# Encoder layer on one core: the down projection's quadrant sums by accumulating DMA, the residual on VectorE, four rows of the final norm in another place

## The chip, the cores and the metric

One core of a Trainium2 chip runs the whole program in one launch. The metric is device time in microseconds (us): the median of several executions. A profile is one such execution, taken by the hardware profiler. Its engines are PE (TensorE, the matmuls), DVE (VectorE), ACT (ScalarE), POOL (GpSimd) and SP (SyncE, which here only issues transfers). Transfers (DMA) run on 16 DMA engines that all queues share; the queue names SPq, ACTq and POOLq say who issued a transfer.

## The reference

One encoder layer on a sequence of 1024 positions and 1024 channels, in float32: a layer norm, a Fourier mixer, a residual with layer norm, a gated MLP with a convolution of three taps over positions, and again a residual with layer norm. The part that the change touches is the end:

```python
def conv_ffn(x, w_up, conv_w, conv_b, w_down):
    h = depthwise_conv(x @ w_up, conv_w, conv_b)
    g, v = jnp.split(h, 2, axis=-1)
    return (jax.nn.silu(g) * v) @ w_down

h = layer_norm(DEEPNORM_ALPHA * h + mix, ln_tok_g, ln_tok_b)
ffn = conv_ffn(h, ff_w_up, ff_conv_w, ff_conv_b, ff_w_down)
h = layer_norm(DEEPNORM_ALPHA * h + ffn, ln_ffn_g, ln_ffn_b)
```

The gated product has 1024 positions and 2816 features; `w_down` is 2816 x 1024. The kernel's outputs are these 1024 x 1024 numbers.

## The kernel before, in words

The up projection makes the gated features in 22 blocks of 128 (index `j`). Each block is convolved by VectorE (`tap`, L1042), passed through SiLU on ScalarE, multiplied with its value half by GpSimd (`conv_done`, L1074) and stored to DRAM in the tensor `gd` by a transfer from ScalarE's queue (`store`).

The down projection multiplies the gated features (A: 1024 positions x 2816 features) by the weight (B: 2816 x 1024). A and B are cut into quadrants, two halves of the features by two halves of positions or of output channels, and the four quadrant products are made with seven multiplications in place of eight, of sums and differences of quadrants. These are the seven stages `s` = 0 to 6. A stage runs over `NK` = 11 feature blocks of 128, taken in pairs: `NB` = 6 steps `b`, the last with one block only (`span(b)`). `order` lists the 42 pairs (s, b).

For each pair there are four steps:

- `down_load` fetches the quadrant pieces that the stage needs, a tile of 128 partitions x 2 x 512 each (512 KB), by transfers on SP's queue (L1089): from `gd` into tiles `qa`, from the weight into tiles `qw`. The running sums of A and of B live in the tiles `sst[b]` and `tst[b]`.
- `down_sums` forms the stage's sums by elementwise instructions (L1129): the weight's on VectorE, the activation's on GpSimd for even `b` and on VectorE for odd `b`.
- `down_prep` splits each sum into a high and a low part for three reduced-precision matmul passes: a cast on ScalarE (L175, tiles `ga` and `wb`), then a subtraction on VectorE (L172).
- `down_mm` runs the matmuls: 4 position blocks x 2 feature blocks x 3 passes (L181, L183, L185), 24 for a full pair, into four PSUM banks `dn`. Stages 0 to 5 add up in two sets of four banks. After a stage, `down_out` adds the set's present content into or out of the residual tiles `acc` on VectorE (L1303), so that each product reaches all the outputs it belongs to.

The steps run ahead of each other by hand: at the turn `n` the loop loads pair n + 3, prepares pair n + 2 and multiplies pair n. Instructions of PE, VectorE, ScalarE and GpSimd run on each engine in the order in which the program writes them; a transfer on SP's queue waits until its tile is free. Nearly all large tiles are taken from one pool of `N4` = 46 buffers.

In `extra` other work is laid between the stages: the convolution of the last feature block, the load of the eight residual tiles `acc` (`load_acc`, 128 rows each), and `residual2`, which scales and shifts each of them, 384 columns on VectorE and 640 on GpSimd (L1171, L1172).

Stage 6 is the last product. It runs row block by row block (banks `dl`), so that rows 0 to 3 can be finished one at a time. Rows 4 to 7 are complete after stage 5. `last_row` makes a row's mean and variance (`bn_aggr`), its reciprocal root on GpSimd (L214, a power) and calls `finish`, which normalizes one part of the columns on VectorE and another on ScalarE and GpSimd (L1265, L1272, L1273) and stores the row. Before, `last_row(4 + rb)` stands after the matmuls of row `rb`, ahead of `last_row(rb)`.

Of the kernel before, what the change touches and what calls it, by code (L numbers as in the profile page):

```python
# [10 lines left out]
F32 = mybir.dt.float32  # L11
# [10 lines left out]
DFF = 2816  # L22
NF = DFF // P
HALF = 512
NFREQ = 514
EPS = 1e-5
ALPHA = 2.0 ** 0.25
# [73 lines left out]
def layout(inp):  # L101
    a = {}
    x = inp["x"][0]
    a["x"] = np.concatenate([x[fold_order()].reshape(8, P, D), x[row_order()].reshape(8, P, D)[1::2]])
    a["winT"] = inp["fn_w_in"][0].T.reshape(G, GD, D)
    wo = inp["fn_w_out"][0].reshape(G, GD, D)
    a["w1"] = wo[:, 1:64].reshape(4, 126, D)
    a["w2"] = wo[:, :64:-1].reshape(4, 126, D)
    e = wo[:, 0:65:64].reshape(16, D)
    we = np.zeros((80, D), e.dtype)  # L110
    for r in (0, 32, 64):
        we[r : r + 16] = e
    a["we"] = we
    up = inp["ff_w_up"][0].reshape(2, KT // 2, P, 2, NF, P)
    a["wup"] = up.transpose(4, 3, 2, 0, 1, 5).reshape(NF, 2, P, D)
    a["wd"] = inp["ff_w_down"][0].reshape(NF, P, D)
    cw = np.concatenate([inp["ff_conv_w"][0], inp["ff_conv_b"][0][None]], axis=0).reshape(4, 2, NF, P)
    a["cols"] = np.concatenate(
        [
            inp["emb_ln_g"].reshape(KT, P).T,  # L120
            inp["fn_b_in"][0].reshape(G, P).T,
            inp["ln_tok_g"][0].reshape(KT, P).T,
            inp["ln_tok_b"][0].reshape(KT, P).T,
            cw.transpose(3, 2, 1, 0).reshape(P, NF * 8),
        ],
        axis=1,
    )
    a["rows"] = np.stack(
        [
            inp["emb_ln_g"],  # L130
            inp["emb_ln_b"],
            inp["fn_b_out"][0],
            inp["ln_tok_g"][0],
            inp["ln_tok_b"][0],
            inp["ln_ffn_g"][0],
            inp["ln_ffn_b"][0],
        ]
    ).reshape(7, 1, D)
    a.update(constants())
    return {k: np.ascontiguousarray(v) for k, v in a.items()}  # L140
# [3 lines left out]
def encoder_layer(ctx: ExitStack, tc: tile.TileContext, a, out: bass.AP):  # L144
# [20 lines left out]
    def raw(ap):  # L165
        return ap.bitcast(F32)
# [7 lines left out]
    def split(hi, lo, src, eng=nc.vector):  # L174
        nc.scalar.copy(out=hi, in_=src)  # L175
        lows(lo, src, hi, eng)
# [860 lines left out]
    prep(0, (4, 3))  # L1037
    prep_b(3, full, ks=(0,))

    gd = dram.tile([NF, P, SEQ], F32, name="gd")  # L1040
    def tap(t, c, w, lo, hi, sh, wi):
        nc.vector.scalar_tensor_tensor(  # L1042
            out=t[:, lo:hi],
# [7 lines left out]
    spill, ct = {}, {}  # L1051

    def store(j):
        nc.scalar.dma_start(out=gd[j], in_=spill.pop(j))

    def conv_taps(j, v, part=range(4)):
        c = cc[j][v]
# [16 lines left out]
        nc.gpsimd.tensor_tensor(out=tg, in0=tg, in1=tv, op=ALU.mult)  # L1074
        spill[j] = tg

    NK = NF // 2
    NB = (NK + 1) // 2
    lo_c, hi_c = hs
    quads, sst, tst, dops = {}, {}, {}, {}  # L1080

    def span(b):
        return min(2, NK - 2 * b)

    def quad(name, src, half, b, c):
        n = span(b)
        t = t4([P, 2, 512], F32, name)
        f0 = half * NK + 2 * b
        nc.sync.dma_start(out=t[:, 0:n], in_=src[f0 : f0 + n, :, c].rearrange("k p c -> p k c"))  # L1089
        return t  # L1090

    def act_quad(i, k, b, s):
        return quad(f"qa{s}{b}", gd, k, b, hs[i])

    def wgt_quad(k, j, b, s):
        return quad(f"qw{s}{b}", a["wd"], k, b, hs[j])

    def down_load(s, b):
        q = quads[s, b] = {}
        if s == 0:  # L1100
            q["a"] = act_quad(0, 0, b, s)
            tst[b] = wgt_quad(0, 0, b, s)
        elif s == 1:
            sst[b] = act_quad(1, 0, b, s)
            q["a"] = act_quad(1, 1, b, s)
            q["b"] = wgt_quad(0, 1, b, s)
        elif s == 2:
            q["a"] = act_quad(0, 0, b, s)
            q["b"] = wgt_quad(1, 1, b, s)
        elif s == 3:  # L1110
            q["a"] = act_quad(1, 1, b, s)
            q["b"] = wgt_quad(0, 0, b, s)
        elif s == 4:
            q["a"] = act_quad(0, 1, b, s)
            q["b"] = wgt_quad(1, 1, b, s)
        elif s == 5:
            q["a"] = act_quad(1, 1, b, s)
            q["b"] = wgt_quad(1, 0, b, s)
        else:
            q["a"] = act_quad(0, 1, b, s)  # L1120
            q["b"] = wgt_quad(1, 0, b, s)

    def down_sums(s, b):
        n = span(b)
        q = quads[s, b]
        ea = nc.gpsimd if b % 2 == 0 else nc.vector

        def tt(eng, o, x, y, op):
            eng.tensor_tensor(out=o[:, 0:n], in0=x[:, 0:n], in1=y[:, 0:n], op=op)  # L1129

        if s == 0:
            return q["a"], tst[b]
        if s == 1:
            tt(ea, sst[b], sst[b], q["a"], ALU.add)
            tt(nc.vector, tst[b], q["b"], tst[b], ALU.subtract)
            return sst[b], tst[b]
        if s == 2:
            tt(ea, sst[b], sst[b], q["a"], ALU.subtract)
            tt(nc.vector, tst[b], q["b"], tst[b], ALU.subtract)
            return sst[b], tst[b]  # L1140
        if s == 3:
            tt(ea, q["a"], q["a"], sst[b], ALU.subtract)
            tt(nc.vector, q["b"], tst[b], q["b"], ALU.subtract)
            return q["a"], q["b"]
        if s == 4:
            tt(ea, q["a"], q["a"], sst[b], ALU.subtract)
            return q["a"], q["b"]
        if s == 5:
            tt(nc.vector, q["b"], q["b"], tst[b], ALU.subtract)
            return q["a"], q["b"]  # L1150
        return q["a"], q["b"]

    def down_prep(s, b):
        n = span(b)
        xa, xb = down_sums(s, b)
        g = [t4([P, 2, 2, 256], F32R, f"ga{s}{b}{l}") for l in range(2)]
        w = [t4([P, 2, 512], F32R, f"wb{s}{b}{l}") for l in range(2)]
        split(g[0][:, 0:n], g[1][:, 0:n], xa[:, 0:n].rearrange("p k (j u) -> p k u j", u=2))
        split(w[0][:, 0:n], w[1][:, 0:n], xb[:, 0:n])
        dops[s, b] = g, w  # L1160

    acc = []
# [3 lines left out]
        nc.sync.dma_start(out=z, in_=h1d[i])  # L1166
        acc.append(z)

    def residual2(i):
        for eng, c in ((nc.vector, slice(0, 384)), (nc.gpsimd, slice(384, 1024))):  # L1170
            eng.tensor_tensor(out=acc[i][:, c], in0=acc[i][:, c], in1=tokg[:, c], op=ALU.mult)  # L1171
            eng.tensor_tensor(out=acc[i][:, c], in0=acc[i][:, c], in1=tokb[:, c], op=ALU.add)  # L1172

    held = {1: 3, 2: 1}
    for j in range(NF):
# [155 lines left out]
    def extra(s, b):  # L1331
        if s == 0:
            if b == 0:
                store(NF - 2)
                conv_taps(NF - 1, 1)
            elif b == 1:
                conv_done(NF - 1)
                for i in range(4):
                    load_acc(i)
                residual2(0)  # L1340
            elif b == 2:
                store(NF - 1)
                for i in range(4, 8):
                    load_acc(i)
                residual2(1)
            else:
                residual2(b - 1)
        elif s == 1:
            if b == 0:
                residual2(5)  # L1350
                down_out(0)
            elif b == 1:
                residual2(6)
            elif b == 2:
                residual2(7)
        elif b == 0 and s < 6:
            down_out(s - 1)
        if s == 5 and b == 1:
            for i in range(4):
                half_stats(i, 1)  # L1360
            for i in range(4, 8):
                half_stats(i, 1)

    for n, (s, b) in enumerate(order[: 6 * NB]):
        if s < 2 and b == 0:
            banks[s] = [bank(f"dn{s}{rb}") for rb in range(4)]
        if n + 3 < len(order):
            down_load(*order[n + 3])
        if n + 2 < len(order):
            down_prep(*order[n + 2])  # L1370
        down_mm(s, b, range(4), banks[s % 2], slice(0, 512), s < 2 and b == 0, b == NB - 1)
        extra(s, b)
        if (s, b) == (4, 0):
            ffg, ffb = row(5, "ffg"), row(6, "ffb")
    for n in range(6 * NB + 2, len(order)):
        if n + 1 < len(order):
            down_load(*order[n + 1])
        down_prep(*order[n])
    for rb in range(4):
        z = acc[4 + rb][:, hs[0]]  # L1380
        nc.vector.tensor_tensor(out=z, in0=z, in1=banks[1][rb], op=ALU.add)
        half_stats(4 + rb, 0)
    for rb in range(4):
        pieces = (slice(0, 512),) if rb < 3 else (slice(0, 256), slice(256, 512))
        for pi, c in enumerate(pieces):
            bk = bank(f"dl{rb}{pi}")
            for b in range(NB):
                down_mm(6, b, (rb,), {rb: bk[:, 0 : c.stop - c.start]}, c, b == 0, b == NB - 1)
            if pi == 0:
                last_row(4 + rb)  # L1390
            z = acc[rb][:, c]
            nc.vector.tensor_tensor(out=z, in0=z, in1=bk[:, 0 : c.stop - c.start], op=ALU.add)
            nc.vector.bn_stats(out=s6[rb][:, 0 if pi == 0 else 2], in_=z)
# [21 lines left out]
```

## Time and profile before

| | us |
|---|---|
| median of three runs | 902.02 (901.75 to 903.17) |
| profiled execution, its own time | 900.76 |
| span in the profile, first to last instruction | 899.0 |
| PE busy | 819.8 |
| VectorE busy | 784.1 |
| GpSimd busy | 450.2 |
| ScalarE busy | 374.1 |
| first weight load and last matmul start of stages 0 to 5 | 635.7 and 854.0 |

Busy time is a sum over the span. Matmuls are pipelined and their ends are modelled, so a busy PE may still run below its peak; the number of matmuls in a stretch, and the clock that it was granted, say more. In the page's slices each digit is the busy share of a fortieth of the span in tenths. A group's row gives the line, engine, operation, output and inputs, count, busy time and mean duration, and behind the second bar the idle time of the engine ahead of these instructions and who ended it.

### The profile page before, as it was taken

How to read it: one execution, taken by the hardware profiler on the slowest of the kernel's cores; microseconds unless marked ns; L12 is line 12 of the kernel's file. 1: busy time of each engine (PE TensorE's matmuls, PEld its weight loads, DVE VectorE, ACT ScalarE, POOL GpSimd, SP SyncE). 2: the span in 40 equal slices, each digit the busy share in tenths (PEclk: the TensorE clock that was granted, in tenths of full speed). 3: DMA queues.
4: the chain of work that ended last, by engine and by line, in shares of the span. 5: the costliest groups of instructions: out<-in, count | busy, mean ns of one | idle time of the engine just before them, and what ended most of it. 6: DMA issues, size and time to landing. Idle time of an engine off the chain costs nothing.

```text
span 899.0 us, 10396 instructions
## 1 busy us (share of the span) xinstructions
PE 819.8 (91%) x3803; PEld 671.4 (75%) x3803; DVE 784.1 (87%) x1000; ACT 374.1 (42%) x572; POOL 450.2 (50%) x254
## 2 busy tenths in 40 slices
PE   8985989967899999999999999999974899999993
PEld 7874968866688788888888888888752677788883
DVE  5998798999897998887888888787999999989975
ACT  4524563564354444444444343444511234244511
POOL 4579597977814633455433455431199222210056
PEclk9997989988999999999999999999997899999998
DMA  9206531221122322222322222336793355477412
GB/s 360 102 1 147 153 140 48 94 94 48 47 71 94 94 94 71 71 70 80 118 84 70 71 71 71 105 103 195 269 331 124 125 175 195 146 259 270 150 71 117
DMA packets 42196, 112.35 MB, mean 125 GB/s; under 512 B 3673, under 2 KB 4569, under 8 KB 42145
## 3 DMA queue, kind: packets, MB, share of 16 engines
q1 hardware_dynamic: 38192, 97.92, 31.8%
q10 hardware_dynamic: 3168, 11.54, 3.2%
q0 software_dynamic: 784, 2.23, 1.0%
q8 instruction: 30, 0.49, 0.2%
q14 instruction: 22, 0.17, 0.1%
HBM read 91.75 MB, written 19.92 MB: 124 GB/s over the span
## 4 chain that ended last, share of the span: by engine, by line
PE 51%; DVE 16%; issue 3%; POOL 3%; ACT 2%; DMA 0%; POOLq 0%; ACTq 0%; DVEq 0%
PE by L181 6%; PE by L185 6%; PE by L183 6%; PE bz L181 4%; PE bz L183 4%; PE bz L185 4%; PE bx L181 4%; PE bx L183 4%; PE bx L185 4%; DVE wb L172 4%; PE dn L183 3%; PE dn L185 3%; PE dn L181 3%; DVE ga L172 2%; DVE t L1042 2%
## 5 line engine op out<-in xcount | busy, mean ns | idle before, releaser
L1074 POOL TENSOR_TENSOR t<-t,t 128x1024 f32<-128x1024 f32 x22 | 54.6, 2483 | 241.1 <-DVE t L1042 198.3
L1042 DVE SCALAR_TENSOR_TENSOR t<-c,cols,t 128x1 f32<-128x1 f32 (+2 forms) x264 | 141.8, 585 | 3.5 <-ACT t L1064 0.5
L181 PE MATMUL dn<-wb,ga 128*128 128x512 f32 x264 | 107.2, 406 | 13.6 <-DVE ga L172 13.6
L183 PE MATMUL dn<-wb,ga 128*128 128x512 f32 x264 | 107.5, 407 | 10.6 <-DVE wb L172 10.5
L181 PE MATMUL by<-b,a 128*128 128x512 f32 (+1 forms) x268 | 106.3, 397 | 3.6 <-DVE c L918 3.6
L185 PE MATMUL dn<-wb,ga 128*128 128x512 f32 x264 | 106.0, 402 | 0.0
L185 PE MATMUL by<-b,a 128*128 128x512 f32 (+1 forms) x268 | 105.6, 394 | 0.0
L183 PE MATMUL by<-b,a 128*128 128x512 f32 (+1 forms) x268 | 105.5, 393 | 0.0
L172 DVE TENSOR_TENSOR a<-s,a 128x512 fp32r<-128x512 f32 x85 | 87.5, 1030 | 18.4 <-ACT a L869 18.4
L175 ACT CAST ga<-qa 128x1024 fp32r<-128x1024 f32 (+1 forms) x42 | 44.1, 1050 | 84.0 <-DVE qa L1129 58.9
L181 PE MATMUL bz<-b,a 128*128 128x512 f32 (+1 forms) x180 | 71.4, 397 | 3.5 <-DVE a L172 3.5
L1129 POOL TENSOR_TENSOR qa<-qa,qa 128x1024 f32<-128x1024 f32 x12 | 35.0, 2912 | 78.1 <-DMA qa<-gd 66.2
L183 PE MATMUL bz<-b,a 128*128 128x512 f32 (+1 forms) x180 | 71.1, 395 | 2.9 <-DVE b L172 2.9
L181 PE MATMUL bx<-b,a 128*128 128x512 f32 (+1 forms) x192 | 72.2, 376 | 1.3 <-ACT c L985 1.3
L183 PE MATMUL bx<-b,a 128*128 128x512 f32 (+1 forms) x192 | 71.9, 374 | 0.0
L185 PE MATMUL bx<-b,a 128*128 128x512 f32 (+1 forms) x192 | 71.9, 374 | 0.0
L181 PEld LDWEIGHTS dn<-wb,ga 128*128 128x128 f32 x264 | 51.1, 193 | 27.7 <-issue 8.3
L183 PEld LDWEIGHTS dn<-wb,ga 128*128 128x128 f32 x264 | 51.1, 193 | 27.0 <-DVE wb L172 15.6
L185 PE MATMUL bz<-b,a 128*128 128x512 f32 (+1 forms) x180 | 71.1, 395 | 0.0
L172 DVE TENSOR_TENSOR a<-wr,a 128x512 fp32r<-128x512 f32 x64 | 70.4, 1102 | 0.4 <-ACT a L869 0.4
L172 DVE TENSOR_TENSOR wb<-qw,wb 128x1024 fp32r<-128x1024 f32 (+1 forms) x42 | 65.9, 1569 | 0.5
L918 DVE TENSOR_TENSOR c<-bz,c 128x512 f32<-128x512 f32 x44 | 30.4, 691 | 39.0 <-PE bz L185 38.3
(332 smaller groups left out, 2036.6 us busy)
## 6 DMA issues: line engine op xcount, KB each, us to landing
wr<-wup SPq DMA_DIRECT2D x44, 512.0 KB, 4.1
qa<-gd SPq DMA_DIRECT2D x40, 512.0 KB, 6.3
qw<-wd SPq DMA_DIRECT2D x35, 512.0 KB, 4.3
gd<-t ACTq DMA_DIRECT2D x22, 512.0 KB, 4.5
winT<-winT SPq DMA_DIRECT2D x8, 512.0 KB, 7.0
x<-x SPq DMA_DIRECT2D x8, 512.0 KB, 11.2
acc<-h1d SPq DMA_DIRECT2D x8, 512.0 KB, 8.0
w<-w SPq DMA_DIRECT2D x8, 504.0 KB
```

The lines of the kernel that those rows point to most:

```text
L172: eng.tensor_tensor(out=lo, in0=src, in1=raw(hi), op=ALU.subtract)
L175: nc.scalar.copy(out=hi, in_=src)
L181: nc.tensor.matmul(outs[i], ll, rh[i], start=first, stop=False, **kw)
L183: nc.tensor.matmul(outs[i], lh, rl[i], start=False, stop=False, **kw)
L185: nc.tensor.matmul(outs[i], lh, rh[i], start=False, stop=last, **kw)
L918: nc.vector.tensor_tensor(out=o, in0=b, in1=x, op=ALU.add)
L1042: nc.vector.scalar_tensor_tensor(out=t[:, lo:hi], in0=c[:, lo + sh : hi + sh], scalar=w[:, wi : wi + 1], in1=t[:, lo:hi], op0=ALU.mult, op ...
L1074: nc.gpsimd.tensor_tensor(out=tg, in0=tg, in1=tv, op=ALU.mult)
L1129: eng.tensor_tensor(out=o[:, 0:n], in0=x[:, 0:n], in1=y[:, 0:n], op=op)
```

## The change

In the down projection the sums are no longer formed by VectorE and GpSimd. A tile is fetched, negated on ScalarE where the formula asks for a difference, and the other operand is added to it by a transfer from GpSimd's queue that accumulates into the tile (`pile`). For the stage 3 sums the source of that transfer is another tile on the chip, otherwise it is DRAM. Stage 2 keeps the sum of A with the opposite sign and takes the sign out again when the weight is split. Between `down_load` and `down_prep` there is a step of its own, `down_pile`, and at turn n the loop loads up to pair n + 5, piles up to n + 4 and prepares up to n + 2, further in stage 5.

The weight and `gd` are laid out in DRAM by quadrant and pair, so that a fetch reads 4 KB in one piece for each partition; a gated block is therefore stored in two halves. The residual (`residual2`) is done on VectorE alone, a half row at a time, over stages 0 to 2, and its tiles are loaded one step earlier. The statistics of the second halves come one step later in stage 5. The final norm of rows 4 to 7 (`last_row`) stands ahead of the last product.

```diff
-    gd = dram.tile([NF, P, SEQ], F32, name="gd")
+    gd = dram.tile([2, 2, NB, P, 2, 512], F32, name="gd")
...
     def store(j):
-        nc.scalar.dma_start(out=gd[j], in_=spill.pop(j))
+        k, b, kk = j // NK, j % NK // 2, j % NK % 2
+        t = spill.pop(j)
+        for h in range(2):
+            nc.scalar.dma_start(out=gd[k, h, b, :, kk], in_=t[:, hs[h]])
...
+    def fetch(name, src, b):
+        t = t4([P, 2, 512], F32, name)
+        nc.sync.dma_start(out=t[:, 0 : span(b)], in_=src)
+        return t
+
+    def pile(t, src):
+        nc.gpsimd.dma_start(out=t[:, 0 : src.shape[1]], in_=src, accum_op=ALU.add)
+
+    def negate(t, b):
+        nc.scalar.mul(t[:, 0 : span(b)], t[:, 0 : span(b)], -1.0)
...
+    def down_load(s, b):
+        g, w = quads_of(b)
+        if s == 0:
+            tst[b] = fetch(f"sb{b}", w(0, 0), b)
+            dsrc[s, b] = fetch(f"qa{s}{b}", g(0, 0), b), tst[b]
+        elif s == 1:
+            sst[b] = fetch(f"sa{b}", g(0, 1), b)
+            dsrc[s, b] = sst[b], tst[b]
+        elif s == 2:
+            dsrc[s, b] = sst[b], tst[b]
+        elif s == 3:
+            dsrc[s, b] = fetch(f"qa{s}{b}", g(1, 1), b), fetch(f"qw{s}{b}", w(0, 0), b)
+        elif s == 4:
+            dsrc[s, b] = sst[b], fetch(f"qw{s}{b}", w(1, 1), b)
+        elif s == 5:
+            dsrc[s, b] = fetch(f"qa{s}{b}", g(1, 1), b), tst[b]
+        else:
+            dsrc[s, b] = fetch(f"qa{s}{b}", g(1, 0), b), fetch(f"qw{s}{b}", w(1, 0), b)
+
+    def down_pile(s, b):
+        g, w = quads_of(b)
         n = span(b)
+        xa, xb = dsrc[s, b]
+        if s == 1:
+            negate(xb, b)
+            pile(xa, g(1, 1))
+            pile(xb, w(0, 1))
         elif s == 2:
+            negate(xa, b)
+            negate(xb, b)
+            pile(xa, g(0, 0))
+            pile(xb, w(1, 1))
         elif s == 3:
+            negate(xb, b)
+            pile(xa, sst[b][:, 0:n])
+            pile(xb, tst[b][:, 0:n])
         elif s == 4:
+            pile(xa, g(1, 0))
         elif s == 5:
+            negate(xb, b)
+            pile(xb, w(1, 0))
 
     def down_prep(s, b):
...
-        split(w[0][:, 0:n], w[1][:, 0:n], xb[:, 0:n])
+        hi, lo = [x[:, 0:n] for x in w]
+        if s == 2:
+            nc.scalar.mul(hi, xb[:, 0:n], -1.0)
+            nc.vector.scalar_tensor_tensor(
+                out=lo, in0=xb[:, 0:n], scalar=-1.0, in1=raw(hi), op0=ALU.mult, op1=ALU.subtract
+            )
+        else:
+            split(hi, lo, xb[:, 0:n])
...
-    def residual2(i):
-        for eng, c in ((nc.vector, slice(0, 384)), (nc.gpsimd, slice(384, 1024))):
-            eng.tensor_tensor(out=acc[i][:, c], in0=acc[i][:, c], in1=tokg[:, c], op=ALU.mult)
-            eng.tensor_tensor(out=acc[i][:, c], in0=acc[i][:, c], in1=tokb[:, c], op=ALU.add)
+    def residual2(i, h):
+        z = acc[i][:, hs[h]]
+        nc.vector.tensor_tensor(out=z, in0=z, in1=tokg[:, hs[h]], op=ALU.mult)
+        nc.vector.tensor_tensor(out=z, in0=z, in1=tokb[:, hs[h]], op=ALU.add)
...
+    def reach(n):
+        i = n - 5 * NB
+        return n + 3 if i < 0 else 5 * NB + (3, 5, 6, 8, 10, 12)[i]
+
+    done = {down_load: 3, down_pile: NB, down_prep: 2}
     for n, (s, b) in enumerate(order[: 6 * NB]):
...
-        if n + 3 < len(order):
-            down_load(*order[n + 3])
-        if n + 2 < len(order):
-            down_prep(*order[n + 2])
+        for step, lead in ((down_load, 3), (down_pile, 2), (down_prep, 0)):
+            while done[step] < min(len(order), reach(n) + lead):
+                step(*order[done[step]])
+                done[step] += 1
         down_mm(s, b, range(4), banks[s % 2], slice(0, 512), s < 2 and b == 0, b == NB - 1)
         extra(s, b)
...
         half_stats(4 + rb, 0)
     for rb in range(4):
+        last_row(4 + rb)
+    for rb in range(4):
         pieces = (slice(0, 512),) if rb < 3 else (slice(0, 256), slice(256, 512))
...
-            if pi == 0:
-                last_row(4 + rb)
```

In `extra` the residual's calls are spread over blocks 2 to 5 of stage 0 (first halves of rows 0 to 3), 1 to 5 of stage 1 (second halves of rows 0 to 3, first halves of rows 4 to 7) and 1 to 4 of stage 2 (second halves of rows 4 to 7).

More of the change, by code (lines that the diff above doesn't have):

```diff
@@ L24 @@
 HALF = 512
+NK = NF // 2
+NB = (NK + 1) // 2
 NFREQ = 514
@@ L115, in layout @@
     a["wup"] = up.transpose(4, 3, 2, 0, 1, 5).reshape(NF, 2, P, D)
-    a["wd"] = inp["ff_w_down"][0].reshape(NF, P, D)
+    wd = inp["ff_w_down"][0].reshape(2, NK, P, 2, 512)
+    wd = np.concatenate([wd, np.zeros((2, 2 * NB - NK, P, 2, 512), wd.dtype)], axis=1)
+    a["wd"] = wd.reshape(2, NB, 2, P, 2, 512).transpose(0, 4, 1, 3, 2, 5)
     cw = np.concatenate([inp["ff_conv_w"][0], inp["ff_conv_b"][0][None]], axis=0).reshape(4, 2, NF, P)
@@ L1075, in conv_done @@
         spill[j] = tg
[L1077 to L1080, printed above, removed]
+    sst, tst, dops, dsrc = {}, {}, {}, {}
     def span(b):
         return min(2, NK - 2 * b)
-    def quad(name, src, half, b, c):
-        n = span(b)
[L1087 to L1106, printed above, removed]
+    def fetch(name, src, b):
+        t = t4([P, 2, 512], F32, name)
+        nc.sync.dma_start(out=t[:, 0 : span(b)], in_=src)
+        return t
@@ new lines, in pile, with quads_of, g, w @@
+    def pile(t, src):
+        nc.gpsimd.dma_start(out=t[:, 0 : src.shape[1]], in_=src, accum_op=ALU.add)
+    def negate(t, b):
+        nc.scalar.mul(t[:, 0 : span(b)], t[:, 0 : span(b)], -1.0)
+    wdq = a["wd"]
+    def quads_of(b):
+        def g(k, h):
+            return gd[k, h, b, :, 0 : span(b)]
+        def w(k, h):
+            return wdq[k, h, b, :, 0 : span(b)]
+        return g, w
+    def down_load(s, b):
[16 more added lines that the diff above has]
+            dsrc[s, b] = fetch(f"qa{s}{b}", g(1, 0), b), fetch(f"qw{s}{b}", w(1, 0), b)
@@ L1107, in down_load @@
+    def down_pile(s, b):
+        g, w = quads_of(b)
+        n = span(b)
+        xa, xb = dsrc[s, b]
[3 more added lines that the diff above has]
+            pile(xb, w(0, 1))
         elif s == 2:
-            q["a"] = act_quad(0, 0, b, s)
-            q["b"] = wgt_quad(1, 1, b, s)
+            negate(xa, b)
+            negate(xb, b)
+            pile(xa, g(0, 0))
+            pile(xb, w(1, 1))
         elif s == 3:
-            q["a"] = act_quad(1, 1, b, s)
@@ L1112, in down_load @@
-            q["b"] = wgt_quad(0, 0, b, s)
+            negate(xb, b)
+            pile(xa, sst[b][:, 0:n])
+            pile(xb, tst[b][:, 0:n])
         elif s == 4:
-            q["a"] = act_quad(0, 1, b, s)
-            q["b"] = wgt_quad(1, 1, b, s)
+            pile(xa, g(1, 0))
         elif s == 5:
[L1117 to L1151, printed above, removed]
@@ L1153, in down_prep @@
+            negate(xb, b)
+            pile(xb, w(1, 0))
     def down_prep(s, b):
         n = span(b)
-        xa, xb = down_sums(s, b)
+        xa, xb = dsrc.pop((s, b))
         g = [t4([P, 2, 2, 256], F32R, f"ga{s}{b}{l}") for l in range(2)]
@@ L1334, in extra @@
                 store(NF - 2)
+                for i in range(4):
+                    load_acc(i)
                 conv_taps(NF - 1, 1)
@@ L1337, in extra @@
                 conv_done(NF - 1)
-                for i in range(4):
+                for i in range(4, 8):
                     load_acc(i)
-                residual2(0)
             elif b == 2:
                 store(NF - 1)
[L1343 to L1347, printed above, removed]
+            for i in ((), (), (0,), (1,), (2,), (3,))[b]:
+                residual2(i, 0)
         elif s == 1:
             if b == 0:
-                residual2(5)
                 down_out(0)
[L1352 to L1356, printed above, removed]
+            else:
+                for i in ((0, 1), (2, 3), (4, 5), (6,), (7,))[b - 1]:
+                    residual2(i, 1 if i < 4 else 0)
+        elif b == 0:
             down_out(s - 1)
-        if s == 5 and b == 1:
+        elif s == 2 and b < 5:
+            residual2(3 + b, 1)
+        if s == 5 and b == 2:
             for i in range(4):
@@ L1374, in encoder_layer @@
             ffg, ffb = row(5, "ffg"), row(6, "ffb")
[L1375 to L1378, printed above, removed]
     for rb in range(4):
```

## The prediction

> **What bounds the kernel now.** I read the page's slices first, then a table of the projection's stages, then the matrix engine's rows, then the shapes by stage.
>
> ```profile
> span 899.0 us, 10396 instructions
> ...
> PE 819.8 (91%) x3803; PEld 671.4 (75%) x3803; DVE 784.1 (87%) x1000; ACT 374.1 (42%) x572; POOL 450.2 (50%) x254
> ...
> PE   8985989967899999999999999999974899999993
> ...
> DVE  5998798999897998887888888787999999989975
> ...
> PEclk9997989988999999999999999999997899999998
> DMA  9206531221122322222322222336793355477412
> ```
>
> A slice is 22.5 us. PE is full from the 12th on, except in slices 30 to 32 (652 to 719 us) and in the last one. Those two holes are what this change can reach.
>
> ```profile
> 500.00:600.00 100.00, 100.00 (x434) 81.10 (x433) 83.41 (x122) 41.26 (x60) 46.27 (x28) 1.00 0.24 79
> ...
> 635.70:660.00 24.30, 22.47 (x96) 17.67 (x95) 23.63 (x26) 11.88 (x13) 11.93 (x5) 1.00 0.73 273
> 660.00:720.00 60.00, 39.86 (x136) 29.07 (x134) 59.64 (x38) 10.71 (x10) 42.86 (x19) 0.83 0.48 171
> 720.00:780.00 60.00, 57.76 (x244) 45.42 (x245) 58.95 (x58) 22.51 (x23) 14.76 (x5) 1.00 0.53 180
> 780.00:854.30 74.30, 74.30 (x322) 60.07 (x321) 67.68 (x70) 36.34 (x39) 4.81 (x2) 1.00 0.62 216
> 854.30:885.10 30.80, 30.80 (x166) 26.30 (x164) 20.97 (x44) 4.75 (x6) 18.94 (x16) 1.00 0.21 83
> ```
>
> The columns are PE, its weight load, DVE, ACT, POOL, then granted clock, DMA share and GB/s. Between 660 and 720 us VectorE is busy 59.64 of 60 us while PE starts 136 matmuls instead of some 260, and the granted clock falls to 0.83. DVE is the bound there; the transfers (0.48) are not.
>
> ```profile
> L181 PEld LDWEIGHTS dn<-wb,ga x264: 186/188/331, 635.7 to 853.3; 128*128 128x128 f32 x132
> ...
> L185 PE MATMUL dn<-wb,ga x264: 387/393/628, 636.4 to 854.0; 128*128 128x512 f32 x132
> L1303 DVE TENSOR_TENSOR acc<-acc,dn x28: 677/679/691, 706.1 to 823.9; 128x512 f32<-128x512 f32 x28
> ...
>   DVE wb L172: 26.1, 22
>   DVE ga L172: 13.6, 6
>   issue: 8.3, 2
> ```
>
> These rows of the products' own answer say the same: PE sat idle until DVE had written a split weight (26.1 us) or activation (13.6 us). Stages 0 to 5 have 3 x 264 = 792 matmuls. At full pace 780 to 854.3 us holds 321 whole ones in 74.3 us, 0.2314 us each, so the six stages cost 792 x 0.2314 = 183.3 us. They begin at 635.7 and could end at 819.0; they end at 854.0 + 0.23, say 854.3. So **35.3 us** are lost to waiting and to the lower clock, and that is the prize.
>
> **The engines' part of the change.** First why DVE is full.
>
> ```profile
> L1129 POOL TENSOR_TENSOR qa<-qa,qa 128x1024 f32<-128x1024 f32 x12 | 35.0, 2912 | 78.1 <-DMA qa<-gd 66.2 <-DVE qw L1129 10.8 <-DVE wb L172 1.2
> L1129 DVE TENSOR_TENSOR qw<-qw,qw 128x1024 f32<-128x1024 f32 (+1 forms) x24 | 30.6, 1274 | 0.0
> L1129 DVE TENSOR_TENSOR qa<-qa,qa 128x1024 f32<-128x1024 f32 (+1 forms) x12 | 15.3, 1278 | 0.0
> L1172 DVE TENSOR_TENSOR acc<-acc,tokb 128x384 f32<-128x384 f32 x7 | 9.7, 1383 | 0.2
> L1171 DVE TENSOR_TENSOR acc<-acc,tokg 128x384 f32<-128x384 f32 x7 | 7.9, 1131 | 0.0
> ```
>
> ```profile
> L172 DVE TENSOR_TENSOR wb<-qw,wb 128x1024 fp32r<-128x1024 f32 x14 | 29.7, 2123 | 0.1
> ...
> L172 DVE TENSOR_TENSOR ga<-qa,ga 128x1024 fp32r<-128x1024 f32 x14 | 21.9, 1565 | 0.4 <-ACT ga L175 0.2
> ```
>
> ```profile
> L172 DVE TENSOR_TENSOR wb<-qw,wb 128x1024 fp32r<-128x1024 f32 x12 | 14.6, 1221 | 0.1
> L172 DVE TENSOR_TENSOR ga<-qa,ga 128x1024 fp32r<-128x1024 f32 x12 | 14.6, 1219 | 1.6 <-ACT ga L175 1.6
> L175 ACT CAST ga<-qa 128x1024 fp32r<-128x1024 f32 x12 | 13.5, 1128 | 7.3 <-DVE qa L1129 6.9 <-PE dn L185 0.4
> ...
> L1323 DVE BATCH_NORM_STATS2 obs<-acc 128x6 f32<-128x512 f32 x12 | 7.6, 684 | 0.1
> ```
>
> ```profile
> 645.08 1.22 DVE L172 TENSOR_TENSOR ga<-qa,ga 128x1024 fp32r<-128x1024 f32 x1
> 646.22 1.22 DVE L172 TENSOR_TENSOR wb<-qw,wb 128x1024 fp32r<-128x1024 f32 x1
> ```
>
> The second fence is 640 to 760 us, the third 800 to 860 us, and the fourth DVE's order of time. The same weight split takes 2123 ns while POOL works and 1221 ns while POOL rests; a 384-wide residual takes 1131 to 1383 ns, though a 512-wide add elsewhere takes 679.
>
> (a) Quadrant sums leave DVE: 24 + 12 instructions, 30.6 + 15.3 = 45.9 us, and 35.0 us leave POOL. In stage 2 the weight's split becomes a product with -1 in one instruction; I take the same 1.22 us.
> (b) The residual becomes 8 rows x 2 halves x 2 = 32 DVE instructions. At 0.68 us that is 21.8 us, against 17.6 us for seven rows now: +1.7 us, and POOL is empty, so the splits fall to 1.22 us.
> (c) DVE then needs two splits, 2.44 us, per block of 24 matmuls (24 x 0.2314 = 5.55 us), 30.55 us a stage. Stage 1 has 11 x 1.22 for its 5.5 blocks, 16 residual instructions and 4 output adds, 13.4 + 10.9 + 2.7 = 27.0 us. Stage 5 is fuller: the new schedule draws nine blocks' splits into it, 22.0 us, beside 4 output adds and the 8 statistics (moved one block later), 2.7 + 5.5, so 30.2 us; its own splits come first, and a spill-over of up to a block would fall on the last product, which has that time (final norm, below). So DVE goes off the path. What is left is the handover at 645 us, where the last taps of the convolution still stand ahead of the third block's splits: those end at 647.4, two blocks of matmuls at 635.7 + 11.1 = 646.8, so 0.7 us, kept.
> (d) ACT gets the negations: 6, 12, 6 and 6 in stages 1, 2, 3 and 5. With 1.13 us each (the cast's row), stage 2 has four ACT instructions a block, 4.5 us of 5.55. That is hidden by the matmuls; uncovered, the 30 would cost 34 us. A negation in stage 3 waits for a weight fetched one block earlier, and behind it in ACT's order stand the casts of the block two ahead: a fetch that takes 8 us (row below) holds ACT 2.5 us, within the two blocks' lead.
> (e) The spill is stored in two halves, 22 more issues on ACT. At 0.33 us (row below) they are 7.3 us over the 22 feature blocks, beside PE that is full (500 to 600 us, ACT 41%): nothing. Without that cover, 7.3 us.
>
> **The DMA part.** Here the trace has no row: nothing in it accumulates.
>
> ```profile
> 620.24 0.33 ACTq L1054 DMA_DIRECT2D gd<-t  x1
> ```
>
> ```profile
> 650.00:655.00 5.00, 3.35 (x15) 2.37 (x13) 5.00 (x6) 0.63 (x2) 4.24 (x2) 1.00 0.99 391
> ```
>
> ```profile
> q0 software_dynamic: 288, 1.05, 27.1%
> ...
> sn<-c_sin POOLq DMA_DIRECT2D x2, 512.0 KB, 6.1
> ```
>
> ```profile
> L505 POOL DMA_DIRECT2D sn<-c_sin x2: 540/560/580, 96.5 to 97.3; - x2
> ```
>
> ```profile
> qa<-gd SPq DMA_DIRECT2D x20, 512.0 KB, 8.3
> ```
>
> ```profile
> 624.81 0.38 SPq L1089 DMA_DIRECT2D qa<-gd  x1
> ```
>
> Per block the seven stages used 2, 3, 2, 2, 2, 2, 2 fetches. Now they use 2, 1, 0, 2, 1, 1, 2 fetches, and 0, 2, 2, 2, 1, 1, 0 accumulating transfers from POOL's queue. POOL issues 48 of them at 0.56 us, 27 us on an engine that the change empties. Each waits there for a negation or a fetch; what queues behind it is the next such transfer alone, since the last gate product stands ahead of them and the final norm behind. The residual's eight loads move one block forward on SP, ahead of stage 1's fetches; they are in the count that follows. A plain 512 KB occupies the 16 engines 524 KB / 391 GB/s = 1.34 us when they are full (650 to 655 us). For an accumulating one the lowest bound is the same 1.34. POOL's plain transfers, between 94 and 108 us and beside others, took 27.1% of 14 us for two, 1.90 each. The upper bound is twice that, 3.80, if the destination is read as well. I take 2 x 1.34 = **2.68 us**, since an add has two operands to fetch: between the ends, nearer to the rows at full load, which is the load that this stage will have.
>
> Demand by the end of stage 3, in 512 KB from the first of these issues at 624.8: fetches 9 + 5.5 + 0 + 11, plus 8 residual rows, 33.5 x 1.34 = 44.9 us; 33 accumulating ones, 88.4 us. They would be through at 758.1. The last (half) block of stage 3 starts on PE at 635.7 + 4 x 30.55 - 2.8 = 755.1, and its casts and splits take 4 us: needed at 751. So the transfers are **7 us late** there, and PE waits that long. Stages 4 and 5 ask 5.5 x (1.34 + 2.68) = 22 us each of 30.55, so nothing is added later. What is new is that a late transfer, not DVE, is next in line.
>
> The price has a page: the Trainium skill, Collectives: The Full Stack, on the bandwidth ceiling, holds that a reducing transfer is slower because it reads two sources, 62.28 against 32.35 GB/s, a factor of 1.93, and that the add itself is free. By that rule an estimate is 2.59 us a transfer and the work is through at 755, 4 us late; by POOL's row alone (1.90) it is through at 732 and nothing is late. No run here shows which holds.
>
> **The final norm.**
>
> ```profile
> 858.82 0.99 POOL L214 TENSOR_TENSOR o4rs<-o4v,small 128x1 f32<-128x1 f32 x1 [57.70 <-DVE o4v L213]
> ...
> 892.44 1.33 POOL L214 TENSOR_TENSOR o3rs<-o3v,small 128x1 f32<-128x1 f32 x1
> ```
>
> From 858.8 on POOL goes through eight rows one after the other, 33.6 us for seven steps, and the last product's matmuls (to 885.1) end before that chain. Putting rows 4 to 7 first changes the order but not the chain: it still begins 4.5 us after stage 5 and still has seven steps at 4.3 to 5.3 us (4.8 in the mean). What is moved ahead of row 0 to 3's adds is, per row, five short DVE instructions, one on ACT, three on POOL and a store on SP; DVE reaches row 0's add when row 7 is through, some 18 us after stage 5, while POOL is still at row 7, so this costs nothing by itself. I take 0, with -2 to +2. The end stays 899.0 - 854.3 = 44.7 us behind stage 5.
>
> **The sum.** 819.0 + 0.7 + 7 = 826.7 for the end of stage 5; + 44.7 = 871.4 span. The profiled execution has 900.76 us for a span of 899.0, so +1.8: 873.2; the median of the runs, 902.02, is 1.3 above that execution: **874.5 us**, 27.5 less.
>
> **Rivals.**
> *Transfers hidden altogether.* At up to 2.46 us each (44.9 + 33 x 2.46 = 126, at 751) nothing is late, PE runs without a gap: 867, with the tail's 2 us 865. For it: POOL's plain row at 1.90 and DMA shares of 0.48 to 0.53 in this stretch now. Against: twice the reading.
> *Transfers become the bound, slower than before.* It decides at the end of stage 3: a delay of 34.6 us eats the prize, which is (751 + 34.6 - 624.8 - 44.9) / 33 = 3.52 us a transfer. At 3.80 they are through at 795, 44 us late: 911. At four plain ones (5.36) they are 96 us late: 963. For it: three stages in a row with 2 such transfers a block, 33 in 91 us, and POOL's rows when mixed with others lie above the plain ones. Against: the full-load rows.
> *The change does not do what it says:* PE stays starved because fetches wait for buffers (two blocks more are loaded ahead, from the same 46), or ACT's order holds the casts; the sums' removal is worth little: 900 to 904. Against: fewer tiles are allocated per block in stages 1, 2, 4 and 5.
>
> **How the numbers follow.** About 0.2% (1.8 us) is what a measurement of this kernel can tell from no change. Forecast (2.46 to 3.3 us a transfer, 866 to 894): 0.46. Hidden: 0.25. Slower through transfers: 0.24. Unmoved: 0.04, and 0.01 for the small rest. Faster 0.71, same 0.04, slower 0.25. The likeliest one's own range is 866 to 894. The whole runs from 860 (hidden, with the tail's gain) to 912 (3.80 us), leaving out the dearest transfers.
>
> **What would show it.** Right: no DVE or POOL rows for the sums; splits near 1.22 us all through; the products' idle time released by a transfer or a cast, mostly in stage 3; DMA share at 0.9 or more in stages 1 to 3; clock 1.00; stage 5 over by about 827; the POOL chain of the norm as long as now. Wrong: transfers of POOL's queue that land later than 11 us (two blocks) after issue in stages 1 and 2 too, which is the slower rival; PE without idle time, which is the hidden one; or a chain of norms shorter by more than 2 us.

## The result, and the profile after

| | before | after |
|---|---|---|
| median, us | 902.24 | 879.77 |
| lowest to highest, us | 901.75 to 903.17 | 879.34 to 881.32 |
| ratio (95% interval) | | 0.9753 (0.9736 to 0.9770) |
| span of the profiled execution, us | 899.0 | 877.9 |

The change makes the kernel 22.5 us faster. The prediction was 874.5 us. First the slices of the changed kernel's page, in the order of the lines shown of the kernel before.

```profile
span 877.9 us, 10479 instructions
...
PE 813.2 (93%) x3803; PEld 668.5 (76%) x3803; DVE 721.1 (82%) x980; ACT 401.8 (46%) x602; POOL 424.6 (48%) x274
...
PE   8984989967799999999999999999999999899992
...
DVE  5999698999988898888888878888696865668856
...
PEclk9997999989899999999999999999999999999997
DMA  9305531131112223322222233222899999999212
```

The hole in PE is closed but for one slice at 8. DVE falls to 5 to 8 from the 31st slice on, where it mostly stood at 9. The transfers, at 3 to 7 before in all but the first of these slices, are at 9 for eight slices: the bound has moved there. The same four stretches as before (PE, weight load, DVE, ACT, POOL, clock, DMA share, GB/s):

```profile
635.70:660.00 24.30, 22.43 (x96) 17.64 (x95) 22.96 (x29) 15.45 (x17) 11.29 (x9) 1.00 0.95 350
660.00:720.00 60.00, 58.61 (x252) 46.97 (x252) 45.62 (x57) 34.48 (x36) 17.91 (x22) 1.00 1.06 238
720.00:780.00 60.00, 55.61 (x230) 43.61 (x229) 36.53 (x42) 29.52 (x31) 14.14 (x17) 0.97 1.07 255
780.00:854.30 74.30, 74.30 (x323) 60.41 (x322) 52.61 (x75) 33.17 (x37) 19.07 (x18) 1.00 0.57 180
```

From 660 to 720 us PE now starts 252 matmuls instead of 136. What it still waits for, in the answer on the products and in PE's order of time (the bracket is the idle time before the instruction and its releaser):

```profile
L185 PEld LDWEIGHTS dn<-wb,ga x264: 186/188/330, 636.4 to 830.6; 128*128 128x128 f32 x132
...
L189 PE MATMUL dn<-wb,ga x264: 387/393/628, 637.0 to 831.3; 128*128 128x512 f32 x132
...
  DVE wb L176: 6.6, 7
  DVE wb L1162: 3.7, 4
  ACT wb L1161: 3.6, 4
```

```profile
655.77 0.50 PE L187 MATMUL dn<-wb,ga 128*128 128x512 f32 x1 [1.79 <-DVE wb L176]
```

```profile
717.67 0.49 PE L185 MATMUL dn<-wb,ga 128*128 128x512 f32 x1 [0.62 <-ACT wb L1161]
718.93 0.50 PE L187 MATMUL dn<-wb,ga 128*128 128x512 f32 x1 [0.76 <-DVE wb L1162]
```

```profile
748.62 0.47 PE L185 MATMUL dn<-wb,ga 128*128 128x512 f32 x1 [2.32 <-DVE ga L176]
749.66 0.50 PE L187 MATMUL dn<-wb,ga 128*128 128x512 f32 x1 [0.57 <-DVE wb L176]
```

Stages 0 to 5 run from 636.4 to 831.5 us, against 635.7 to 854.3. Going by the starts of the matmuls, 2.0 us are lost at the handover from the up projection (656 us), 3.7 us in the second half of stage 2 (717 to 727 us, two such pairs), and 3.3 us in stage 3 (749 us). Of the other 2.8 us, 0.2 are a first short wait at the handover (648 us) and some 1.6 lie behind that last wait, where the granted clock fell to 0.66 and five us show 16 matmuls instead of the 23 of a stretch at full clock:

```profile
750.00:755.00 5.00, 5.00 (x16) 3.95 (x15) 5.00 (x9) 2.62 (x3) 2.50 (x5) 0.66 1.04 271
```

In the rows of PE above, L176, L1161 and L1162 are instructions of the split; behind them stand the transfers, as the waits of all engines from 625 to 880 us show:

```profile
ACT ga L179 <- DMA sa<-gd: 14.6, 10, 5.0
ACT wb L179 <- DMA sb<-wd: 14.0, 10, 2.8
ACT wb L1161 <- DMA sb<-wd: 10.1, 5, 3.8
```

The full-sized splits themselves are at 1.22 us (640 to 830 us), but for one at the handover that took 3.40 us. The row of one kind:

```profile
L176 DVE TENSOR_TENSOR ga<-sa,ga 128x1024 fp32r<-128x1024 f32 x15 | 18.3, 1222 | 10.5 <-ACT ga L179 10.3
```

And the price that no row of before had: in stages 1 and 2, where GpSimd's accumulating queue runs alone, the answer on transfers from 662 to 696 us gives the following (queue, packets, MB, share of 16 engines over the window):

```profile
q0 software_dynamic: 2075, 7.05, 105.6%
```

7.05 MB are 13.4 transfers of 512 KB; 1.056 x 34 us / 13.4 = 2.67 us of all 16 engines for one, at 207 GB/s counted by the bytes added. The share adds up the times of all packets and so can pass 100%; by bytes and rate alone one transfer takes 524 KB / 207 GB/s = 2.53 us.

The chain of the final norm, first and last power on POOL:

```profile
835.41 1.00 POOL L218 TENSOR_TENSOR o4rs<-o4v,small 128x1 f32<-128x1 f32 x1 [35.70 <-DVE o4v L217]
...
868.83 1.33 POOL L218 TENSOR_TENSOR o3rs<-o3v,small 128x1 f32<-128x1 f32 x1
```

33.4 us, against 33.6 before.

### The profile page after: what moved, and what is told of

The parts are those of the page before. It is cut to its first block, busy times and chain, and to the rows that moved or that the text cites. A ratio compares the mean times of both kernels' runs of the same rounds, so it can differ in the third digit from the quotient of the medians.

```text
span 877.9 us, 10479 instructions
## 1 busy us (share of the span) xinstructions
PE 813.2 (93%) x3803; PEld 668.5 (76%) x3803; DVE 721.1 (82%) x980; ACT 401.8 (46%) x602; POOL 424.6 (48%) x274
## 5 line engine op out<-in xcount | busy, mean ns | idle before, releaser
L187 PE MATMUL dn<-wb,ga 128*128 128x512 f32 x264 | 105.2, 398 | 4.0 <-DVE wb L176 2.4
L185 PE MATMUL dn<-wb,ga 128*128 128x512 f32 x264 | 105.0, 398 | 3.7 <-DVE ga L176 2.3
L189 PE MATMUL dn<-wb,ga 128*128 128x512 f32 x264 | 104.5, 396 | 0.0
L176 DVE TENSOR_TENSOR a<-s,a 128x512 fp32r<-128x512 f32 x85 | 88.7, 1043 | 14.9 <-ACT a L873 14.6
L176 DVE TENSOR_TENSOR a<-wr,a 128x512 fp32r<-128x512 f32 x64 | 71.5, 1120 | 1.9 <-ACT a L873 1.9
L185 PEld LDWEIGHTS by<-b,a 128*128 128x128 f32 x268 | 51.3, 191 | 16.1 <-DVE c L922 4.9
L187 PEld LDWEIGHTS dn<-wb,ga 128*128 128x128 f32 x264 | 49.9, 189 | 17.8 <-DVE wb L176 4.2
L185 PEld LDWEIGHTS dn<-wb,ga 128*128 128x128 f32 x264 | 50.0, 189 | 16.3 <-ACT wb L179 2.7
L1230 ACT COPY c<-bx 128x512 f32<-128x512 f32 x22 | 12.9, 587 | 104.7 <-DVE c L922 104.7
L189 PEld LDWEIGHTS by<-b,a 128*128 128x128 f32 x268 | 51.2, 191 | 11.6
```

The costliest lines, as they stand in the source:

```text
L176: eng.tensor_tensor(out=lo, in0=src, in1=raw(hi), op=ALU.subtract)
L185: nc.tensor.matmul(outs[i], ll, rh[i], start=first, stop=False, **kw)
L187: nc.tensor.matmul(outs[i], lh, rl[i], start=False, stop=False, **kw)
L189: nc.tensor.matmul(outs[i], lh, rh[i], start=False, stop=last, **kw)
L1230: nc.scalar.copy(out=cg[:, 0:512], in_=bx[j])
```

## The experiments

Ten kernels ran, each timed against the kernel before on the same chip. Their ratios are to that kernel; the changed kernel's is 0.9753.

**What the accumulation costs.** GpSimd's transfers as plain copies, the addition left out:

```diff
-        nc.gpsimd.dma_start(out=t[:, 0 : src.shape[1]], in_=src, accum_op=ALU.add)
+        nc.gpsimd.dma_start(out=t[:, 0 : src.shape[1]], in_=src)
```

> The changed kernel with GpSimd's 48 transfers as plain copies: same bytes, same waits, same negations, but the addition is left out. Theory (an accumulating 512 KB takes 2.5 to 2.7 us of all DMA engines, twice a plain one, and this fills them in stages 1 to 3): GpSimd's queue falls to 1.3 to 1.9 us for 512 KB, the waits of the matmuls in stages 2 and 3 go, stage 5 ends some 8 to 9 us earlier, 870 to 873 us. Rival (the transfers are late through their fixed latency and order, not through the engines' time): GpSimd's queue takes less, but the waits stay, 877 to 881 us.

Measured: 872.07 us (870.18 to 872.38), ratio 0.9661 (0.9647 to 0.9675). The same window of its transfers:

```profile
q0 software_dynamic: 2937, 10.61, 84.1%
```

10.61 MB are 20.2 transfers, 0.841 x 34 / 20.2 = 1.41 us each. Accumulating costs 2.67 / 1.41 = 1.89 times the engine time of a plain copy by the same queue. Going by the rates of all queues with the engines full it is 1.95 times: 413 GB/s with the plain copies (662 to 674 us), 212 GB/s in the changed kernel (662 to 696 us). And the matmuls lose 2.4 us in all, nearly all of it at the handover:

```profile
660.00:720.00 60.00, 60.00 (x260) 48.59 (x259) 53.52 (x69) 40.52 (x45) 13.84 (x26) 1.00 0.88 319
720.00:780.00 60.00, 60.00 (x261) 48.72 (x260) 41.26 (x44) 35.40 (x39) 9.06 (x17) 1.00 0.79 282
```

The negations and the order of the issues were the same. An issue took GpSimd 0.53 us instead of 0.87 or more, but GpSimd had time to spare in both kernels: it stood waiting for ScalarE's negations for over 75 us. So it is the engines' time that makes the transfers late, as the theory had it.

**No sums at all.** The 48 transfers left out, and so all sums:

```diff
     def pile(t, src):
-        nc.gpsimd.dma_start(out=t[:, 0 : src.shape[1]], in_=src, accum_op=ALU.add)
+        pass
```

> The changed kernel with GpSimd's 48 transfers left out, and with them all sums; negations, splits and matmuls are as they were. It shows the time if the sums cost nothing. Theory: no wait of the matmuls in stages 1 to 3 but the handover near 650 us, stage 5 over by 820 to 823 us, 867 to 871 us in all, which means that the accumulating transfers cost 9 to 12 us. Rival (ScalarE's order and the buffers hold the matmuls up anyway): 876 us or more.

Measured: 868.41 us (867.88 to 870.62), ratio 0.9629 (0.9614 to 0.9645), stage 5 over at 822.2 us, 2.4 us lost in waits. The prediction's case of hidden transfers, 867, comes nearest to this kernel. The accumulating transfers cost 11 us against it, some 2.5 of them behind the last store (last section).

**The layout alone**, on the kernel before:

```diff
-        nc.sync.dma_start(out=t[:, 0:n], in_=src[f0 : f0 + n, :, c].rearrange("k p c -> p k c"))
+        nc.sync.dma_start(out=t[:, 0:n], in_=src[half, h, b, :, 0:n])
...
-        nc.scalar.dma_start(out=gd[j], in_=spill.pop(j))
+        for h in range(2):
+            nc.scalar.dma_start(out=gd[k, h, b, :, kk], in_=t[:, hs[h]])
```

> The kernel before with the new layout alone: weight and gated features by quadrant and pair, 4 KB pieces in a fetch, 22 more stores; sums, residual and norm as before. Theory (VectorE bounded the stage): 900 to 904 us, as the kernel before. Rival (the longer pieces bring a part of the gain): 893 to 898 us.

Measured: 902.88 us (901.92 to 904.15), ratio 1.0007 (0.9999 to 1.0016). No part of the gain on this kernel; the 22 further stores cost nothing that shows. VectorE holds this kernel up, though, so the run cannot say what the old layout would cost the changed kernel, where the DMA engines are the bound. That was not tried.

**The norm's place.** `last_row(4 + rb)` back behind the matmuls of row `rb`:

```diff
-    for rb in range(4):
-        last_row(4 + rb)
...
+            if pi == 0:
+                last_row(4 + rb)
```

> The changed kernel with the final norm of rows 4 to 7 back in its old place, each row behind the matmuls of one row of the last product. Theory (the end hangs on GpSimd's chain of eight rows, whatever their order): 878 to 882 us, as the changed kernel's 879.8, with the first to the last of the eight power instructions 33 to 34 us apart. Rival (the new place is a part of the gain): slower by 4 us or more, 884 or above.

Measured: 880.82 us (880.28 to 882.54), ratio 0.9771 (0.9757 to 0.9784). The chain, with the rows taken alternately:

```profile
835.13 1.00 POOL L218 TENSOR_TENSOR o4rs<-o4v,small 128x1 f32<-128x1 f32 x1 [37.86 <-DVE o4v L217]
841.04 0.99 POOL L218 TENSOR_TENSOR o0rs<-o0v,small 128x1 f32<-128x1 f32 x1 [1.12 <-DVE o0v L217]
...
869.46 1.33 POOL L218 TENSOR_TENSOR o3rs<-o3v,small 128x1 f32<-128x1 f32 x1
```

34.3 us instead of 33.4, with a 1.1 us gap before row 0, which has to wait for its product. The new place is worth about 1 us at most: the two intervals overlap.

**The norm on VectorE** for all rows but row 3, so that GpSimd has only the powers:

```diff
-        n = 512 if i != 3 else 832
+        n = 1024 if i != 3 else 832
...
-        nc.scalar.activation(out=z[:, d], in_=z[:, d], func=AF.Identity, scale=rs, bias=nb)
+        if i == 3:
+            nc.scalar.activation(out=z[:, d], in_=z[:, d], func=AF.Identity, scale=rs, bias=nb)
```

and likewise for the two GpSimd instructions behind it.

> The changed kernel with the final norm of all rows but row 3 wholly on VectorE (1024 columns in two instructions, in place of 512 there and 512 on ScalarE and GpSimd). Theory (GpSimd's chain of eight rows sets the end: the last power starts 7 us after the last matmul): the chain is gone, the last power starts 1.5 to 2.5 us after the last matmul, 873 to 876 us. Rival (the end hangs on VectorE or on the stores): 878 us or more.

Measured: 875.23 us (874.12 to 876.64), ratio 0.9703 (0.9690 to 0.9716).

```profile
837.16 1.53 POOL L218 TENSOR_TENSOR o4rs<-o4v,small 128x1 f32<-128x1 f32 x1 [37.02 <-DVE o4v L217]
...
865.90 1.25 POOL L218 TENSOR_TENSOR o3rs<-o3v,small 128x1 f32<-128x1 f32 x1 [3.50 <-DVE o3v L217]
```

The chain is 28.7 us long, POOL now waits for VectorE before each row, and the last power starts 1.9 us after the last matmul's end (864.0) instead of 6.5 us (862.3). So GpSimd's chain, not the rows' order, set the end.

**The residual on both engines** again, 192 and 320 columns of each half row:

```diff
+        m = 512 * h + 192
+        for eng, c in ((nc.vector, slice(512 * h, m)), (nc.gpsimd, slice(m, 512 * h + 512))):
+            eng.tensor_tensor(out=acc[i][:, c], in0=acc[i][:, c], in1=tokg[:, c], op=ALU.mult)
+            eng.tensor_tensor(out=acc[i][:, c], in0=acc[i][:, c], in1=tokb[:, c], op=ALU.add)
```

> The changed kernel with the residual shared by VectorE and GpSimd again, 192 and 320 columns of each half row. Theory: VectorE's instructions grow beside GpSimd's (a split above 2 us instead of 1.22 in stages 0 and 1), GpSimd has some 30 us more, and its transfers are issued later; the matmuls wait 2 to 8 us more, 882 to 888 us. Rival (the residual's place does not matter, once the sums are gone from VectorE): 878 to 881 us.

Measured: 879.61 us (879.36 to 881.10), ratio 0.9754 (0.9741 to 0.9768): no change. The theory missed.

```profile
660.00:720.00 60.00, 55.29 (x228) 43.40 (x227) 58.05 (x58) 35.78 (x38) 47.40 (x51) 0.97 1.06 233
720.00:780.00 60.00, 59.39 (x255) 47.53 (x254) 40.34 (x46) 28.28 (x30) 19.11 (x22) 1.00 1.06 260
```

Its mechanism is there: VectorE is full again in the first stretch (58.05 of 60) and PE falls to 228 matmuls from 252. But in the next PE starts 255 instead of 230. By the starts of the matmuls 11.3 us are lost in all, against 11.7 in the changed kernel counted the same way; 6.0 of them are waits between 694 and 709 us, and only 1.2 us are lost in stage 3. The places of the waits suggest that the transfers caught up while PE waited for VectorE; no run takes the two apart. On this reading two waits in one stretch of a stage do not add when a third party, here the DMA engines, works on through both.

**Whose order holds stage 3.** The negation of the fetched weight on GpSimd in place of ScalarE:

```diff
-            negate(xb, b)
             pile(xa, sst[b][:, 0:n])
+            nc.gpsimd.tensor_scalar(out=xb[:, 0:n], in0=xb[:, 0:n], scalar1=-1.0, scalar2=None, op0=ALU.mult)
             pile(xb, tst[b][:, 0:n])
```

> The changed kernel with stage 3's six negations of the weight on GpSimd in place of ScalarE. ScalarE sat 5.8 us in such a negation waiting for the fetch, and the casts of an earlier pair stood behind it. If that order makes the wait at 748 us: ScalarE's wait goes, 875 to 877 us. If the full DMA engines make it: 879 to 882 us, and the split at that place waits for its transfer instead.

Measured: 880.38 us (879.49 to 881.12), ratio 0.9759 (0.9746 to 0.9772): no change. ScalarE did sit in that negation in the changed kernel:

```profile
745.16 1.06 ACT L1098 ACTIVATE qw<-qw 128x1024 f32<-128x1024 f32 x1 [5.75 <-DMA qw<-wd]
```

but with that wait on another engine the matmuls still lost 10.6 us, the handover's 2.0 and the rest from 719 to 763. Stage 3 lost some 3.4 us instead of 5.3, but stage 2 lost 4.8 instead of 4.0, with one wait of 2.7 us at 722: the split that PE waits for there (L1162, at 719.19 us) took VectorE 2.93 us instead of 1.22, beside a negation that takes GpSimd 3.5 us. So this run brings a loss of its own and does not say cleanly what the order on ScalarE is worth. The plain copies say more. There the order is the old one, ScalarE still waits in these negations,

```profile
ACT qw L1098 <- DMA qw<-wd: 9.6, 4, 3.7
```

and no matmul of stages 1 to 5 waits. The order alone does no harm when the transfers are on time; whether it adds to their lateness stays open.

**Fewer accumulating transfers.** Stage 3's weight sums on VectorE, ahead of the split, with no negation:

```diff
-            negate(xb, b)
             pile(xa, sst[b][:, 0:n])
-            pile(xb, tst[b][:, 0:n])
...
+        if s == 3:
+            nc.vector.tensor_tensor(out=xb[:, 0:n], in0=tst[b][:, 0:n], in1=xb[:, 0:n], op=ALU.subtract)
```

> The changed kernel with the weight sums of stage 3 on VectorE again (6 instructions just ahead of their split, no negation and no transfer for them). Theory (the DMA engines are the bound in stages 1 to 3 and VectorE has room: busy 20 of 34 us in stage 3): 5.5 transfers of 2.6 us go, 14 us of the engines, for 6.7 us of VectorE; the waits in stage 3 (some 5 us with the low clock) go, 873 to 876 us. Rival (VectorE's order brings the wait back): 880 us or more.

Measured: 874.13 us (872.27 to 876.97), ratio 0.9694 (0.9674 to 0.9713). The waits of stage 3 are gone, 1.7 us in stage 2 and the handover are left (4.2 us in all):

```profile
720.00:780.00 60.00, 58.75 (x253) 47.13 (x252) 51.00 (x57) 34.86 (x37) 11.86 (x14) 1.00 1.06 277
```

VectorE takes 51.0 us here instead of 36.5 and stays below its limit.

**Both together**, this one and the norm on VectorE:

> Both edits that made the changed kernel faster: stage 3's weight sums on VectorE, and the final norm of all rows but row 3 on VectorE. Theory (they act at different places, the end of stage 5 and the chain behind it, so they add): 874.1 - 879.8 = -5.7 and 875.2 - 879.8 = -4.6, so 869 to 871 us. Rival (with stage 5 over earlier the end is set by VectorE's rows, which take as long): 873 to 875 us.

Measured: 869.92 us (869.07 to 872.62), ratio 0.9654 (0.9638 to 0.9670). The gains add. It is 32 us below the kernel before and 10 us below the changed one.

**Stage 2's weight sums on VectorE as well** (their pieces fetched plainly instead, `fetch(f"qw{s}{b}", w(1, 1), b)`):

> As before it, and the weight sums of stage 2 on VectorE as well: 5.5 accumulating transfers of 2.6 us become plain fetches of 1.3 us, VectorE gets 6.7 us more in stage 2, where it was busy 19 of 30 us. Theory (DMA engines are the bound up to the end of stage 2, and one wait of 1.7 us is left there): no wait but the handover near 657 us, 867 to 870 us. Rival (VectorE's order, with the output adds, takes the place of the transfers): 871 us or more.

Measured: 870.61 us (868.66 to 871.80), ratio 0.9648 (0.9633 to 0.9664), no different from the last. Its profile still shows 6.1 us lost: 2.0 at the handover and 3.2 in single waits from 682 to 721 us, nearly all behind VectorE's splits. The theory's clean stages did not come, and the time lies between the two ranges. Whether VectorE's order took the transfers' place, as the rival had it, is not shown: from 680 to 722 us ScalarE's casts waited 11.9 us for VectorE's sums, but 10.2 us for transfers, and the DMA engines were still full (their share was above 1.0 from 662 to 722 us).

## Why the prediction was right, and where it was off

Direction and mechanism held. PE had been held up, mostly by VectorE (35.3 us lost); the sums left it; transfers took its place as the next bound, in stages 2 and 3. The prize was cut by their lateness, not eaten. No run separates one part of the change, the longer lead (loads up to pair n + 5 instead of n + 3). It can hardly be the cause by itself: in the kernel before, VectorE was busy for 209.9 us between 635.7 and 854.3 us (the four stretches added up), more than the 183.3 us that the matmuls need. But the kernel before with the longer lead was not tried.

The sum gave a span of 871.4 us and the trace has 877.9. The median is nearer to its forecast (5.3 us off instead of 6.5) by luck: the profiled execution lies 0.1 us below the median this time and lay 1.3 below it before. Term by term, in us:

| term | predicted | measured |
|---|---|---|
| start of stage 0's weight loads | 635.7 | 636.4 |
| matmuls of stages 0 to 5 at full pace | 183.3 | 183.3 |
| handover at 645 to 656 | 0.7 | 2.2 |
| transfers late, with the slower clock behind | 7 | 9.6 |
| end of stage 5 | 826.7 | 831.5 |
| from there to the end | 44.7 | 46.4 |

*The accumulating transfer*, the one term without a row, was taken at 2.68 us and measured 2.67 where its queue ran alone; over 620 to 880 us it is 2.66:

```profile
q0 software_dynamic: 6912, 23.07, 45.1%
```

(0.451 x 260 us / 44.0 transfers.) These two are packet times, while the 1.34 us behind the forecast were bytes over rate, and by that measure the accumulating transfer took 2.53 us. So the price was right within 6%, and the agreement to a hundredth is luck. The rule from the Trainium skill that stood beside it (Collectives: The Full Stack, in the section on the bandwidth ceiling: a reduce-scatter reads two sources and an all-gather one, a factor of 1.93) agrees with the trace in its size: 1.89 between the accumulating and the plain copies here, or 1.95 by the rates. That a second read makes the factor, no run shows. POOL's plain row of before (1.90 us beside other transfers), which would have made the transfers vanish from the sum, was not the price of a plain copy in this stage: those took 1.41 us.

*The lateness* was 9.6 us for 7, and began earlier: 3.7 us in stage 2 already, where the prediction had put no wait, then 3.3 in stage 3 and some 1.6 of slower clock behind that wait, which the sum had not priced. That the two waits add up to the 7 us of the sum is luck. With 2.53 us a transfer the same count is through at 753, only 2 us late. But it took the DMA engines as full from 624.8 us on, while they moved 331 GB/s and not 391 up to 654.5 us, which costs 4.5 us; and it left out the stores of the last gated blocks, 1.5 MB on ScalarE's queue by 751 us, some 4 us of the engines at a plain transfer's 1.34 us. Together that is about the lateness seen. This is a count, and no run takes the two out.

*The handover* was 2.2 for 0.7. Part (c) kept only the wait for the third block's splits, which measured 0.2. It missed the next one, of 2.0: POOL's last gate product, which the change does not touch, runs beside a weight split there, and that split takes 3.40 us instead of 1.22; before, the same split took 3.41. First the changed kernel's split and gate product, then the split of the kernel before:

```profile
652.32 3.40 DVE L176 TENSOR_TENSOR wb<-sb,wb 128x1024 fp32r<-128x1024 f32 x1
```

```profile
651.48 3.15 POOL L1081 TENSOR_TENSOR t<-t,t 128x1024 f32<-128x1024 f32 x1 [7.90 <-ACT ga L179]
```

```profile
651.64 3.41 DVE L172 TENSOR_TENSOR wb<-qw,wb 128x1024 fp32r<-128x1024 f32 x1
```

*Part (b), the residual*, was cheap as said, but not the help that was claimed: with POOL taking its old share again the time is the same.

*Part (d)* said that a late fetch would hold ScalarE for 2.5 us without harm. It held it for 5.75, and the weight's fetches of stages 3, 4 and 6 land in 9.8 to 17.3 us instead of 8. In the kernel with plain copies such holds of up to 3.7 us did no harm; for the 5.75 it stays open, since the negation on GpSimd brought a loss of its own.

*Part (e)*, the 22 further stores, costs nothing that shows, as said. *The final norm* was put at 0 with -2 to +2; it is about 1 us of gain at most, not clear of the noise. The tail is longer all the same, by 1.7 us: the chain starts 3.9 us behind stage 5 (4.5 before) and is as long, but from the last store's issue to the end of the span 5.3 us pass instead of 2.8 (last section). Of the signs named ahead, one misled: transfers that land later than two blocks, 11 us, were to mean the slower rival. They do land in 12 to 16 us (medians), and the kernel is still faster. GpSimd issues them well ahead of PE's pace: seven transfers by 661 us, while PE was in stage 0. One issue took it 0.87 us or more, and not the 0.56 of the forecast's part on transfers; it had the room.

## What to carry to other kernels

An accumulating transfer takes an elementwise sum off a full compute engine for nearly twice a plain transfer's time on the DMA engines, so count the stage's transfers against its matmul time first, with that factor, and move only as many sums as fit: here the kernel with 5.5 fewer of them was some 5.5 us faster. When a full engine is relieved, look for the serial chain that comes next (GpSimd's norms), because moving work inside such a chain brought 1 us at most here, while giving it to the engine just relieved brought 4.5. Waits that a stage has for two different reasons need not add, so an edit can measure zero although its mechanism is plainly there. And an edit that measures zero may have brought a new loss of its own, as the negation on GpSimd did: look for it in the trace before calling the mechanism harmless.

## What the runs showed of the hardware that was not expected

The end of the span comes later where GpSimd issues the 48 transfers, accumulating or not. SP's last store and the span, first of the changed kernel, then of the one without these transfers:

```profile
872.62 0.33 SPq L1284 DMA_DIRECT2D out<-acc  x1
```

```profile
863.32 0.33 SPq L1284 DMA_DIRECT2D out<-acc  x1
```

```profile
span 866.1 us, 10352 instructions
```

From that issue to the end it is 5.3 us in the first and 2.8 in the second. In the kernels before and with the layout alone, without the 48, it is 2.8 and 2.9; with all 48 it is 5.2 to 5.6 (the plain copies 5.3), with 42 of them 4.8 and 4.9, with 36 it is 4.3. So it grows with their number. SP waits there for PE's queue (2.6 us at the longest in the changed kernel). What PE's queue does in that time was not tried and stays open.

A negation of one input on GpSimd took 2.8 to 3.8 us for 128 x 1024, around three times ScalarE's 1.05; VectorE was at work beside it, and what it takes alone no run shows. The power instruction of a single column took 0.55 us while VectorE stood waiting for it (changed kernel) and 1.5 us beside VectorE's instructions of 1.27 us (norm on VectorE). And the same code ahead of the projection ended anywhere between 636.2 and 638.8 us in these profiled executions, so a difference of 2 us between two single spans says nothing without the repeated times.
